# A macaron encoder layer in split float32: the order of the matmul passes inside the FFN's block products

## The chip, the cores and the metric

The kernel runs on one core of a Trainium2 chip. A core has a matrix engine (TensorE, PE in the profile, with a separate row PEld for loading its stationary operand), a vector engine (DVE), a scalar engine (ACT), a general engine (POOL), and queues that start transfers (SP's above all). Matmul results go to PSUM, eight banks of 512 float32 per partition; everything else works from the on-chip SBUF, which is loaded from HBM by DMA. The engines run side by side, each through its own queue in order, and wait for each other by semaphores.

The metric is the device time of one execution in microseconds (us), and lower is better. Times come from runs of the same program; a profile is one further execution, recorded instruction by instruction.

## The reference

One layer on 256 frames of width 2048, all in float32:

```python
def swiglu(h, w1, w3, w2):
    return (jax.nn.silu(h @ w1) * (h @ w3)) @ w2
...
x = x + 0.5 * swiglu(rmsnorm(x, ffn1_norm_g[l]), ffn1_w1[l], ffn1_w3[l], ffn1_w2[l])
h = rmsnorm(x, mix_norm_g[l])
proj = h @ w_in[l]
...
merged = jax.nn.sigmoid(ga) * (y_a @ w_branch_a[l]) + jax.nn.sigmoid(gb) * (y_b @ w_branch_b[l])
x = x + merged @ w_out[l]
x = x + 0.5 * swiglu(rmsnorm(x, ffn2_norm_g[l]), ffn2_w1[l], ffn2_w3[l], ffn2_w2[l])
```

The inner width of the FFN is 5632. Between the two FFNs stand two attention branches (differential attention and latent attention) and their projections. This case touches only the two FFNs.

## The kernel before

**Precision.** A float32 product is made from three passes of TensorE. Every operand is split into a high part in the format `fp32r` and a low part, the remainder (`split`, L118 to L121: ACT casts the high part, L120; DVE subtracts it from the source, L121). A product adds high times high, high times low and low times high into the same accumulator. Activations are split once, ahead of time (`T[:, 0]` is the high part and `T[:, 1]` the low part, the stationary operands); weights are split as they arrive.

**Blocks.** The FFN's matrices are multiplied in 2 x 2 blocks by `gemm2` (L293). One call computes a 256 x 1024 result as four blocks of 128 x 512, and adds up over *pairs* of 128-deep slices of the inner dimension. A pair is of one of two kinds:

- "S": seven products of 128 x 128 by 128 x 512 instead of eight (Strassen's scheme in Winograd's form, the table `SEVEN`, L253). It needs sums of weight blocks, which DVE makes (L318 to L320), and two splits: `s`, of the four blocks themselves (one sum takes the place of one of them), and `w`, of three sums. 21 passes.
- "P": the plain eight products (`PLAIN`, L255), arranged so that they go into four of the same accumulators. One split, `p`. 24 passes.

The seven accumulators `q1` to `q7` are one PSUM bank each; the eighth bank is for transposes. `q1`, `q6` and `q7` get products of S pairs only, so they are emptied right after the last S pair of the call (L335 to L343); `q5`, `q2`, `q3` and `q4` are emptied after the last pair (L346 to L355), by DVE operations of 512 columns that add them into the SBUF tile `ev` or, in the last down calls, into `x`.

**Buffers of weights.** A pair's weights come by two DMAs of 512 KB each on SP's queue into a tile `raw` (L313, L314); there are three `raw` tiles, three `wh` (high) and three `wl` (low). An S pair uses one `raw` and two of each of the others. A `raw` tile is free when its pair's split is done.

**Order of passes.** The helper `three` (L303) issues the three passes of one product one after another: high-high, high-low, low-high. The program gives the instructions this order and a planner may move an instruction ahead of others whose operands are not ready in the planner's own reckoning; what an engine really runs is seen in the trace.

**Calls.** `ffn` (L378) goes over 11 groups of 512 inner columns. Each group makes one *up* call over the eight pairs of the width (kinds `TKINDS` = P S P P S P S P, L359): `w1` and `w3` together, then Silu (ACT, L394) and the multiplication (DVE, L395). The result is put into the list `pend` as small steps to be transposed (`put_pairs`, L260: two `turn` steps that transpose on PE, then `sums`, which makes the sums and splits of the stationary operands); `gemm2` runs one such step after each pair, and all that are left before pair number `due`. After groups 2, 5, 8 and 10 two *down* calls follow, for the two halves of the output (`DOWN`, L362: the groups 0-2, 3-5, 6-7, 8-10; two pairs each, of kinds `GKINDS`). The results of the first three are added to `x_mid` in HBM by a POOL DMA with accumulation (L415); the last adds them onto the `x` that was loaded back (`load_x`, L385).

So each FFN has 11 up calls and 8 down calls, and the whole kernel 38 calls of `gemm2`.

## Time and profile before

| | us |
|---|---|
| median of 3 runs | 2462.64 (2459.66 to 2463.09) |
| the profiled execution | 2461.4 |
| its span | 2459.6 |
| first FFN, from the first to the last weight pass in its PE rows | 11.9 to 749.0 |
| second FFN, the same | 1722.8 to 2454.8 |

How the rows are read: PE's matmul rows overlap, because a matmul starts while the one before still drains; a 512-column pass is shown as 0.39 us long while the next starts 0.227 us later. A busy PE is therefore not PE at its peak, and a loss shows as a larger distance of starts or as the idle time in brackets at the end of a row, with the instruction that ended it. In the groups, the number behind the second bar is the idle time of the engine directly before instructions of that group. In the windows the columns are length, busy time of each engine with its count of instructions, then the granted TensorE clock (1.00 is full), the busy share of the DMA engines and GB/s. The tiles are named by the call: `f_u_...` belongs to up calls, `f_d_...` to down calls; `hp`, `lp`, `hs`, `ls`, `hw`, `lw` are the high and low parts of the splits `p`, `s` and `w`.

### The profile page before, as it was taken

Reading aid. Unit: us, or ns where it says so; the run is one execution under the profiler, and the core shown is the slowest. Engines: PE = TensorE matmul, PEld = TensorE weight load, DVE = VectorE, ACT = ScalarE, POOL = GpSimd, SP = SyncE. Lnnn points to the kernel's source line nnn. Section 1 sums busy time; section 2 is a strip of 40 time slices with the busy share of each in tenths; the row PEclk is TensorE's granted clock in tenths of the full one; section 3 lists DMA queues with packets and bytes.
Section 4 is the critical chain, followed back from the end, with each engine's and each line's share of the span. In section 5 each row is a group of like instructions: output and inputs, shape, how many; then the busy total and the mean of one; then the engine's idle time right before and its main releaser. Section 6 shows DMA issues by size and latency. Waiting matters only on the chain.

```text
span 2459.6 us, 28650 instructions
## 1 busy us (share of the span) xinstructions
PE 2401.8 (98%) x10788; PEld 1956.4 (80%) x10788; DVE 1866.9 (76%) x2363; ACT 1241.1 (50%) x1290; POOL 133.8 (5%) x177
## 2 busy tenths in 40 slices
PE   7999999999999999999999999999999999999999
PEld 6887887787888888888878878888777787788787
DVE  7987887888896666756665664556888898788798
ACT  5554554554554455545545544444554455455453
POOL 2000000000000100001121210000000000000000
PEclk9999999999999999999999999999999999999999
DMA  7567567567675555555454445565656665756765
GB/s 245 185 198 226 194 197 211 193 201 206 204 237 178 187 171 171 171 158 170 142 169 146 153 160 184 188 229 195 211 192 205 206 200 178 220 195 199 207 221 171
DMA packets 240490, 471.88 MB, mean 192 GB/s; under 512 B 15012, under 2 KB 28000, under 8 KB 240096
## 3 DMA queue, kind: packets, MB, share of 16 engines
q1 hardware_dynamic: 233280, 446.30, 55.8%
q0 software_dynamic: 6064, 23.10, 4.1%
q8 instruction: 85, 1.39, 0.2%
q10 hardware_dynamic: 1008, 0.66, 0.1%
q14 instruction: 53, 0.43, 0.0%
HBM read 449.02 MB, written 20.97 MB: 191 GB/s over the span
## 4 chain that ended last, share of the span: by engine, by line
PE 25%; issue 23%; POOL 2%; DVE 2%; ACT 1%; DMA 1%; POOLq 0%; SPq 0%; DVEq 0%; ACTq 0%
PE f_u_q L305 3%; PE f_d_q L305 2%; PE ms L557 1%; PE wo L161 1%; PE wo L159 1%; PE wo L160 1%; PE bb L160 1%; PE bb L159 1%; PE bb L161 1%; PE gb L160 1%; PE gb L159 1%; PE gb L161 1%; PE ba L159 1%; PE ba L160 1%; PE ba L161 1%
## 5 line engine op out<-in xcount | busy, mean ns | idle before, releaser
L305 PE MATMUL f_d_q<-f_d_hp,f_gp 128*128 128x512 f32 x960 | 306.7, 395 | 1.6 <-DVE f_u_e L348 1.5
L120 ACT CAST f_u_hp<-f_u_w 128x2048 fp32r<-128x2048 f32 x110 | 210.4, 1912 | 148.3 <-PE f_u_q L305 90.9
L305 PE MATMUL f_u_q<-f_u_hp,hT1p 128*128 128x512 f32 x880 | 283.5, 395 | 0.8 <-ACT f_u_hp L120 0.6
L305 PE MATMUL f_u_q<-f_u_hp,hT2p 128*128 128x512 f32 x880 | 279.9, 391 | 1.5 <-DVE f_u_e L348 0.9
L121 DVE TENSOR_TENSOR f_u_lp<-f_u_w,f_u_hp 128x2048 fp32r<-128x2048 f32 x110 | 251.5, 2286 | 38.5 <-ACT f_u_hp L120 38.5
L120 ACT CAST f_u_hs<-f_u_w 128x2048 fp32r<-128x2048 f32 x66 | 126.1, 1911 | 190.4 <-DVE f_u_w L319 161.9
L305 PEld LDWEIGHTS f_d_q<-f_d_hp,f_gp 128*128 128x128 f32 x960 | 182.3, 190 | 41.7 <-issue 4.0
L305 PE MATMUL f_d_q<-f_d_lp,f_gp 128*128 128x512 f32 x480 | 190.6, 397 | 15.5 <-DVE f_d_lp L121 15.4
L121 DVE TENSOR_TENSOR f_u_ls<-f_u_w,f_u_hs 128x2048 fp32r<-128x2048 f32 x66 | 151.2, 2292 | 62.3 <-ACT f_u_hs L120 62.3
L305 PEld LDWEIGHTS f_u_q<-f_u_hp,hT1p 128*128 128x128 f32 x880 | 167.1, 190 | 38.4 <-issue 2.9
L305 PEld LDWEIGHTS f_u_q<-f_u_hp,hT2p 128*128 128x128 f32 x880 | 165.0, 188 | 38.7 <-issue 4.1
L305 PE MATMUL f_u_q<-f_u_lp,hT1p 128*128 128x512 f32 x440 | 174.2, 396 | 7.3 <-DVE f_u_lp L121 7.3
L305 PE MATMUL f_u_q<-f_u_lp,hT2p 128*128 128x512 f32 x440 | 172.5, 392 | 6.6 <-DVE f_u_lp L121 6.5
L120 ACT CAST f_d_hp<-f_d_w 128x2048 fp32r<-128x2048 f32 x60 | 114.8, 1913 | 63.4 <-PE f_d_q L305 36.6
L121 DVE TENSOR_TENSOR f_d_lp<-f_d_w,f_d_hp 128x2048 fp32r<-128x2048 f32 x60 | 136.9, 2285 | 12.0 <-ACT f_d_hp L120 11.9
L305 PEld LDWEIGHTS f_d_q<-f_d_lp,f_gp 128*128 128x128 f32 x480 | 91.5, 191 | 39.3 <-DVE f_d_lp L121 20.7
L121 DVE TENSOR_TENSOR f_u_lw<-f_u_s,f_u_hw 128x1536 fp32r<-128x1536 f32 x66 | 115.6, 1751 | 0.0
L120 ACT CAST f_d_hs<-f_d_w 128x2048 fp32r<-128x2048 f32 x28 | 53.6, 1913 | 110.5 <-DVE f_d_w L319 85.0
L305 PEld LDWEIGHTS f_u_q<-f_u_lp,hT1p 128*128 128x128 f32 x440 | 83.6, 190 | 29.0 <-DVE f_u_lp L121 12.1
L305 PEld LDWEIGHTS f_u_q<-f_u_lp,hT2p 128*128 128x128 f32 x440 | 82.6, 188 | 27.2 <-DVE f_u_lp L121 10.7
L159 PE MATMUL da<-da_h,hTm 128*128 128x512 f32 x256 | 104.2, 407 | 0.0
L121 DVE TENSOR_TENSOR da_l<-da_w,da_h 128x1024 fp32r<-128x1024 f32 x64 | 76.6, 1221 | 34.6 <-ACT da_h L120 34.3
(385 smaller groups left out, 5673.3 us busy)
## 6 DMA issues: line engine op xcount, KB each, us to landing
f_u_w<-in_ffn_w SPq DMA_DIRECT2D x352, 512.0 KB, 4.7
f_d_w<-in_ffn_w SPq DMA_DIRECT2D x176, 512.0 KB, 5.0
da_w<-in_w_in SPq DMA_DIRECT2D x64, 512.0 KB, 4.5
dav_w<-in_w_in SPq DMA_DIRECT2D x32, 512.0 KB, 4.5
ga_w<-in_w_in SPq DMA_DIRECT2D x32, 512.0 KB, 4.4
ba_w<-in_w_branch_a SPq DMA_DIRECT2D x32, 512.0 KB, 4.9
gb_w<-in_w_in SPq DMA_DIRECT2D x32, 512.0 KB, 4.5
bb_w<-in_w_branch_b SPq DMA_DIRECT2D x32, 512.0 KB, 4.6
```

The lines of the kernel that those rows point to most:

```text
L120: nc.scalar.copy(out=hi, in_=src)
L121: nc.vector.tensor_sub(out=lo, in0=src, in1=hi.bitcast(F32))
L159: nc.tensor.matmul(out=o, lhsT=hi(kb, t), rhs=wh[:, j], start=first, stop=False)
L160: nc.tensor.matmul(out=o, lhsT=hi(kb, t), rhs=wl[:, j], start=False, stop=False)
L161: nc.tensor.matmul(out=o, lhsT=lo(kb, t), rhs=wh[:, j], start=False, stop=last)
L305: nc.tensor.matmul(out=q[o], lhsT=x, rhs=b, start=o not in started, stop=end)
L557: nc.tensor.matmul(out=sp[:, c0:c1], lhsT=q[:, qc:qc + P], rhs=k[:, 0:n], start=i == 0, stop=i == len(blocks) - 1)
```

## The change

It changes only the two FFNs. The count of matmuls, the weight bytes and the splits stay the same.

1. *Passes of a pair.* The helper `passes` takes all products of a pair. Except for the pairs noted, it issues first all passes with the high part of the weights (high-high and low-high of every product) and then all passes with the low part. In an S pair it does so for the four `s` products and then for the three `w` products. The first pair of a call, and a last pair of kind P, go product by product, as before, though with the low part of the weights third.
2. *Accumulators emptied 1024 wide.* `q2` and `q3` become the two halves of one two-bank tile `q23` and are added in one operation; where the result stays in `ev`, the two subtractions from `q5` become one operation.
3. *Pairs reordered.* Up calls other than an FFN's first run in the order `UP` (S P P S P S P P); `GKINDS` becomes PS, SP, PP, with group 7 kept as two P pairs; in a down call the first S pair is moved to the front (S P S P P P, S P P P, and S P P P S P for the last).
4. *Transposes.* A `wait` step in front of `put_pairs` moves each of its steps behind one more pair. The first half of `x` is loaded at once, no longer as steps of `pend`.

```diff
-                split(T[:, 0], T[:, 1], g[:, :n])
+                split(T[:, 0, :n], T[:, 1, :n], g[:, :n])
...
-        q = {k: pools["acc"].tile([P, NW], F32, tag=k, bufs=1, name=f"{name}_{k}") for k in ("q1", "q2", "q3", "q4", "q5", "q6", "q7")}
+        q = {k: pools["acc"].tile([P, NW], F32, tag=k, bufs=1, name=f"{name}_{k}") for k in ("q1", "q4", "q5", "q6", "q7")}
+        q23 = pools["acc"].tile([P, 2, NW], F32, tag="q23", bufs=1, name=f"{name}_q23")
+        q["q2"], q["q3"] = q23[:, 0], q23[:, 1]
...
-        def three(o, T, slot, bh, bl, stop):
-            for x, b, end in ((T[:, 0, slot], bh, False), (T[:, 0, slot], bl, False), (T[:, 1, slot], bh, stop)):
-                nc.tensor.matmul(out=q[o], lhsT=x, rhs=b, start=o not in started, stop=end)
+        nS = sum(p[0] == "S" for p in pairs)
+        left = {o: 3 * nS + (6 * (n - nS) if o in ("q2", "q3", "q4", "q5") else 0) for o in q}
+
+        def passes(T, prods, in_turn):
+            high = lambda o, s, bh, bl: [(o, T[:, 0, s], bh), (o, T[:, 1, s], bh)]
+            low = lambda o, s, bh, bl: [(o, T[:, 0, s], bl)]
+            todo = [m for p in prods for f in (high, low) for m in f(*p)] if in_turn else \
+                [m for f in (high, low) for p in prods for m in f(*p)]
+            for o, x, b in todo:
+                left[o] -= 1
+                nc.tensor.matmul(out=q[o], lhsT=x, rhs=b, start=o not in started, stop=left[o] == 0)
                 started.add(o)
...
-                for o, slot, b, u in SEVEN:
-                    three(o, T, slot, B[b][0][:, u], B[b][1][:, u], o in ("q1", "q6", "q7") and i == lastS)
+                for part in (("sw",) if i == 0 else ("s", "w")):
+                    passes(T, [(o, slot, B[b][0][:, u], B[b][1][:, u]) for o, slot, b, u in SEVEN if b in part], i == 0)
...
-                for o, slot, right_side in [(o, s, 1 - l) for o, s, l in PLAIN]:
-                    for j in range(2):
-                        u = 3 * j if right_side else 1 + j
-                        three(o, T, slot + j, ph[:, u], pl[:, u], i == n - 1 and j == 1)
+                units = [(o, slot + j, 1 + j if l else 3 * j) for o, slot, l in PLAIN for j in range(2)]
+                passes(T, [(o, slot, ph[:, u], pl[:, u]) for o, slot, u in units], i in (0, n - 1))
...
-        nc.vector.tensor_sub(out=e12, in0=q["q5"], in1=e12)
         if x is None:
-            nc.vector.tensor_sub(out=e22, in0=q["q5"], in1=e21)
-            x11, x12, x21 = e11, e12, e21
+            nc.vector.tensor_tensor(out=ev[:, :, NW:], in0=q["q5"].unsqueeze(1).to_broadcast([P, 2, NW]),
+                                    in1=ev.rearrange("p t n -> p (t n)")[:, NW:3 * NW].rearrange("p (a n) -> p a n", a=2),
+                                    op=ALU.subtract)
+            x1, x21 = ev[:, 0], e21
         else:
+            nc.vector.tensor_sub(out=e12, in0=q["q5"], in1=e12)
...
-        nc.vector.tensor_add(out=x11, in0=q["q2"], in1=x11)
-        nc.vector.tensor_add(out=x12, in0=q["q3"], in1=x12)
+            x1 = x[:, 0]
+        nc.vector.tensor_add(out=x1, in0=q23.rearrange("p a n -> p (a n)"), in1=x1)
...
-    TKINDS, GKINDS = "PSPPSPSP", ("PS", "PP", "SP")
+    TKINDS, GKINDS = "PSPPSPSP", ("PS", "SP", "PP")
+    UP = (1, 0, 2, 4, 3, 6, 5, 7)
...
-            ev = gemm2(rows(w1, g * NW), rows(w3, g * NW), T, f"{name}_u{g}", due=5 if g == 0 else None)
+            ev = gemm2(rows(w1, g * NW), rows(w3, g * NW), [T[i] for i in UP] if g else T, f"{name}_u{g}", due=5 if g == 0 else None)
...
-            later(*put_pairs(G[g], lambda t, ev=ev: ev[:, t, 0:NW], None, f"{name}{g}"))
+            if g == 7:
+                G[g] = [("P", v, kb) for _, v, kb in G[g]]
+            later(wait, *put_pairs(G[g], lambda t, ev=ev: ev[:, t, 0:NW], None, f"{name}{g}"))
...
-                pend[0:0] = [partial(load_x, t, 0) for t in range(NT)]
+                for t in range(NT):
+                    load_x(t, 0)
...
             pairs = [p for i in DOWN[g] for p in G[i]]
+            pairs.insert(0, pairs.pop([p[0] for p in pairs].index("S")))
```

The tile of the FFN's stationary operands (`ffn_T`) is also written so that P pairs beyond five would lie behind the S pairs; there are five, so nothing moves.

More of the change, by code (lines that the diff above doesn't have):

```diff
@@ L288, in sums, with gemm2 @@
                     n = 6
-                split(T[:, 0], T[:, 1], g[:, :n])
+                split(T[:, 0, :n], T[:, 1, :n], g[:, :n])
         return [partial(turn, t) for t in range(NT)] + [sums]
-    def gemm2(left, right, pairs, name, due=None, x=None):
-        q = {k: pools["acc"].tile([P, NW], F32, tag=k, bufs=1, name=f"{name}_{k}") for k in ("q1", "q2", "q3", "q4", "q5", "q6", "q7")}
+    def gemm2(wleft, wright, pairs, name, due=None, x=None):
+        q = {k: pools["acc"].tile([P, NW], F32, tag=k, bufs=1, name=f"{name}_{k}") for k in ("q1", "q4", "q5", "q6", "q7")}
+        q23 = pools["acc"].tile([P, 2, NW], F32, tag="q23", bufs=1, name=f"{name}_q23")
+        q["q2"], q["q3"] = q23[:, 0], q23[:, 1]
         ev = pools["ev"].tile([P, NT, 2 * NW], F32, tag="ev", bufs=1, name=f"{name}_e")
@@ L312, in gemm2 @@
             raw = wtile("raw", F32, f"{name}_w")
-            nc.sync.dma_start(out=raw[:, 0::3], in_=right(k))
-            nc.sync.dma_start(out=raw[:, 1:3], in_=left(k))
+            nc.sync.dma_start(out=raw[:, 0::3], in_=wright(k))
+            nc.sync.dma_start(out=raw[:, 1:3], in_=wleft(k))
             h4 = lambda m: (wtile("wh", F32R, f"{name}_h{m}"), wtile("wl", F32R, f"{name}_l{m}"))
@@ L370, in ffn_T @@
         nP = len(TKINDS) - nS
-        tS = pair_views(big.tile([P, nS * 14, P], F32R, tag=tagS, name=f"{name}s"), nS, 7)
-        tP = pair_views(big.tile([P, nP * 12, P], F32R, tag=tagP, name=f"{name}p"), nP, 6)
+        n1, n2 = min(nP, 5), max(nP - 5, 0)
+        b1 = big.tile([P, nS * 14 + n2 * 12, P], F32R, tag=tagS, name=f"{name}s")
+        tS, tP = pair_views(b1, nS, 7), pair_views(b1[:, nS * 14:], n2, 6)
+        tP += pair_views(big.tile([P, n1 * 12, P], F32R, tag=tagP, name=f"{name}p"), n1, 6)
         return [(k, v, 2 * i) for i, (k, v) in enumerate(with_kinds(TKINDS, tS, tP))]
```

## The prediction, made before the changed kernel was run

> **What bounds the kernel now.** I read the page's busy times, then its costliest groups, then the busy times of single calls of `gemm2`, then the order of time around one stall.
>
> ```profile
> span 2459.6 us, 28650 instructions
> PE 2401.8 (98%) x10788; PEld 1956.4 (80%) x10788; DVE 1866.9 (76%) x2363; ACT 1241.1 (50%) x1290; POOL 133.8 (5%) x177
> ...
> L305 PE MATMUL f_d_q<-f_d_lp,f_gp 128*128 128x512 f32 x480 | 190.6, 397 | 15.5 <-DVE f_d_lp L121 15.4
> ...
> L305 PE MATMUL f_u_q<-f_u_lp,hT1p 128*128 128x512 f32 x440 | 174.2, 396 | 7.3 <-DVE f_u_lp L121 7.3
> L305 PE MATMUL f_u_q<-f_u_lp,hT2p 128*128 128x512 f32 x440 | 172.5, 392 | 6.6 <-DVE f_u_lp L121 6.5
> ```
>
> PE is the bound. What it loses in the FFNs stands in front of the low passes (rows with `lp` as moving operand): 15.5 + 7.3 + 6.6 = 29.4 us of idle time, released by the DVE subtraction that makes the low part (L121). No other L305 group loses more than 2 us. So a reorder can win only where PE stands still; the number of matmuls stays the same.
>
> The pitch of an undisturbed stream comes from two rows of the order of time; between them lie 12 matmuls (each product is high, low, high):
>
> ```profile
> 395.85 0.39 PE L305 MATMUL f_d_q<-f_d_lp,f_gp 128*128 128x512 f32 x1
> ...
> 398.57 0.39 PE L305 MATMUL f_d_q<-f_d_lp,f_gp 128*128 128x512 f32 x1
> ```
>
> 2.72 / 12 = 0.2267 us. An up call has 183 matmuls (3 S pairs of 21, 5 P pairs of 24): 41.5 us. A down call over six pairs has 138: 31.3 us; over four pairs 93: 21.1 us. Against this stand the calls by busy time (L305 alone). First the second down pass of each group set and the up call behind it, 12 calls in both FFNs; then, as a second answer, all other up calls but the two first; then the two first:
>
> ```profile
> 382.85:417.48 34.63, 32.07 (x140) 25.59 (x138) 1.00 0.72 214
> 417.48:462.24 44.76, 42.35 (x184) 34.11 (x184) 1.00 0.72 212
> 570.61:596.26 25.65, 23.41 (x94) 18.36 (x93) 0.93 0.77 220
> ...
> sum 455.85, PE 429.93 PEld 344.92; mean PE 35.83 PEld 28.74
> ```
> ```profile
> 639.26:682.13 42.87, 42.48 (x184) 34.12 (x184) 1.00 0.61 203
> ...
> sum 605.94, PE 597.14 PEld 474.67; mean PE 42.65 PEld 33.90
> ```
> ```profile
> 11.92:66.62 54.70, 49.31 (x183) 36.60 (x184) 0.97 0.69 241
> 1722.83:1768.23 45.40, 43.12 (x183) 33.83 (x184) 1.00 0.66 217
> ```
>
> The 12 calls have 4 x 138 + 2 x 93 + 6 x 183 = 1836 matmuls, 416.2 us by the pitch; they take 455.85, so **39.6 us are lost, 3.3 a call**. The 14 others take 605.94 against 14 x 41.5 = 580.9: 25 us, 1.8 a call, and about 0.9 of that are their eight transposes, which the 12 do not have. The calls that lose much are those after a down pass. Why, shows one of them:
>
> ```profile
> 398.14 1.23 DVE L318 TENSOR_TENSOR f_d_s<-f_d_w 128x1024 f32<-128x1024 f32 x1 [4.46 <-DMA f_d_w<-in_ffn_w]
> ...
> 398.79 0.61 PE L305 MATMUL f_d_q<-f_d_hp,f_gp 128*128 128x512 f32 x2
> 399.29 2.29 DVE L121 TENSOR_TENSOR f_d_lp<-f_d_w,f_d_hp 128x2048 fp32r<-128x2048 f32 x1
> 401.49 0.69 DVE L319 TENSOR_TENSOR f_d_w<-f_d_s,f_d_w 128x512 f32<-128x512 f32 x1
> ...
> 401.63 0.50 PE L305 MATMUL f_d_q<-f_d_lp,f_gp 128*128 128x512 f32 x1 [2.22 <-DVE f_d_lp L121]
> ```
> ```profile
> f_d_w<-in_ffn_w SPq DMA_DIRECT2D x6, 512.0 KB, 6.5
> f_u_w<-in_ffn_w SPq DMA_DIRECT2D x6, 512.0 KB, 4.3
> x_mid<-f_d_e POOLq DMA_DIRECT2D x1, 1024.0 KB, 10.7
> ```
> ```profile
> PE f_d_q L305 <- DVE f_d_lp L121: 15.4, 11, 2.8
> ```
>
> After each down pass POOL adds 1 MB into `x_mid` (L415). Beside it the weight loads land after 6.5 us, not 4.3 (the DMA rows of 383 to 412 us). In DVE's queue the sums of the next S pair (L318) stand ahead of this P pair's low part; they wait 4.46 us for their load, the low part waits behind them, and PE, which has run two high passes, stands still for 2.2 us. The load itself is not late for its own pair; it is late for the one queued behind it. The last row, from the view of waits, gives the worst case: 11 such waits of PE in the down calls, the longest 2.8 us.
>
> **The change part by part.**
>
> *High passes first.* A P pair that is neither first nor last now gives PE 16 high passes, 16 x 0.2267 = 3.6 us, before it needs the low part; today it has one or two. The longest wait for a low part, 2.8 us, fits in. In an S pair eight high passes come first (1.8 us), then four low ones. The high tile is also free eight passes earlier, 1.8 us, for ACT's next cast. *Pairs reordered:* each call but the two first up calls starts with its S pair, so the S load that was late (fifth of six) is now first and third. A load is issued when DVE is through with the pair three before it (three `raw` tiles), so both S loads are asked for before the store begins; beside it load the late P pairs, which PE reaches two to three pairs, over 10 us, later. Of the 39.6 us I leave 0.7 a call for its first pair and what is late next (a first S pair that waits for DVE): 8.4. **Term a: -31 us.**
>
> The first up call has the same stall inside (30.71 us, 1.83 idle), and a slow clock behind it. The third number from the end is the granted clock:
>
> ```profile
> 32.10:35.50 3.40, 3.40 (x10) 2.62 (x9) 3.33 (x4) 0.03 (x1) 0.00 (x0) 0.50 0.94 332
> ...
> 2107.40:2110.80 3.40, 3.40 (x9) 2.62 (x9) 2.01 (x3) 2.89 (x2) 0.00 (x0) 0.50 0.69 208
> 401.60:405.00 3.40, 3.37 (x15) 2.78 (x16) 1.99 (x3) 2.67 (x2) 0.00 (x0) 1.00 0.60 195
> ```
> ```profile
> 30.71 0.50 PE L305 MATMUL f_u_q<-f_u_lp,hT1p 128*128 128x512 f32 x1 [1.83 <-DVE f_u_lp L121]
> ...
> 2107.21 0.65 PE L305 MATMUL f_d_q<-f_d_lp,f_gp 128*128 128x512 f32 x1 [2.68 <-DVE f_d_lp L121]
> ```
>
> A 3.4 us stretch at half clock costs 1.7 us. Stall and stretch give **term b: -3.5 us**. The stretches of the 12 calls are inside term a already. [...]
>
> *Ordinary call starts.* The first pair now begins with q1, q6, q7, emptied long before, where it began with q5, emptied last. I take 0.1 us a call off the 20 calls that are not in a: **term c: -2 us**.
>
> *Accumulators 1024 wide.* Before, each is one operation of 512:
>
> ```profile
> L346 DVE TENSOR_TENSOR f_d_e<-f_d_q,f_d_e x16: 680/682/692, 182.8 to 2451.2; 128x512 f32<-128x512 f32 x16
> ```
>
> Two of them take 1.36 us, one 1024 wide 1.23 by L318's row above (from SBUF; a 1024-wide read of PSUM is not in the trace; bounds 0.68 and 1.36). In 34 calls two are saved, in four one: 72 x 0.13 = 9 us of DVE. DVE is 76% busy and these run beside the last passes, so 0 on the path. If the cover goes (the last call), 0.3 us either way. q2's bank is now held until q3 is read too; the next S pair needs q2 only as its fifth product, 12 passes (2.7 us) in: 0.
>
> *Transposes one pair later.* They stop waiting for the activation at a call's start, but a down call needs the last group's operands at its fifth pair. Today the chain runs:
>
> ```profile
> 361.60 0.60 ACT L272 ACTIVATE pf_f<-tp_f 128x512 f32<-128x512 f32 x1
> ...
> 367.09 1.08 DVE L121 TENSOR_TENSOR f_gs<-pf_f,f_gs 128x896 fp32r<-128x896 f32 x1
> ```
>
> 6.6 us from the second transpose to the last low part, with one pair more to spare. After the change one P pair, 24 x 0.2267 = 5.4 us, lies between: 0 to 1.2 us late, in six calls. I take 0.5: **term d: +3 us**. The x loads issued at once, and group 7 kept as P pairs, move nothing that PE waits for: the loads land a whole call ahead, and the pair counts stay 5 P and 3 S, 4 P and 2 S, 3 P and 1 S: 0. The part between the FFNs is not touched.
>
> Sum: -31 - 3.5 - 2 + 3 = -33.5. The profiled execution took 2461.4 us, 1.8 outside its span; 2461.4 - 33.5 = 2428. The median of the runs is 2462.64, 1.2 above it: **2429 us**.
>
> **The rivals.**
>
> 1. *All small waits go too.* Then the 12 calls end near the pitch (-38), the 14 up calls lose half of what is not transposes (-6), b and the down calls add -6: 2462.6 - 50 = **2412**. For it: DVE has no wait left in front of it. Against: first and last pairs still run product by product.
> 2. *The wait only moves.* The last pair of a call runs in turn, so it has no 3.6 us; if the next S pair's L318 stands ahead of its low part as above, half of term a stays (-16), c goes, d costs its upper end (6 x 1.2 = +7) and b -3.5, starts +0: about -13, **2449**. Against: by then the store has ended.
> 3. *Slower: S first starves every call's start.* An S pair needs 1.23 + 2 x 0.69 + 2.29 + 1.75 = 6.6 us of DVE before its last low part, and at a call's start DVE empties accumulators first. The first row, of the page's groups, has the last summand; the others show a call that begins with S today:
>
> ```profile
> L121 DVE TENSOR_TENSOR f_u_lw<-f_u_s,f_u_hw 128x1536 fp32r<-128x1536 f32 x66 | 115.6, 1751 | 0.0
> ...
> 2388.44 0.69 DVE L354 TENSOR_TENSOR f_u_e<-f_u_q,f_u_e 128x512 f32<-128x512 f32 x1
> ...
> 2389.05 2.28 DVE L121 TENSOR_TENSOR f_d_ls<-f_d_w,f_d_hs 128x2048 fp32r<-128x2048 f32 x1
> ...
> 2391.39 0.50 PE L305 MATMUL f_d_q<-f_d_ls,f_gs 128*128 128x512 f32 x1 [0.27 <-DVE f_d_ls L121]
> ```
>
> The subtraction ran behind L354 and PE lost 0.27 us, after hoisting six high passes. 36 calls will start so. It decides from 33.5 / 36 = 0.93 us a call; at the whole 2.28 us it is +82 - 33.5: **2511**. Against: before a call's start now lie two or three P pairs, 2.29 us of DVE each against 5.4 of PE, where here lay one.
> 4. *Nothing happens.* PE's rows show high passes hoisted already, so the order that runs is not the order written; if it comes out alike, **2462**.
> 5. *Banks.* Low passes now change the accumulator on nearly every pass. If that made PE idle in gaps and halved its clock, each 3.4 us stretch would cost 1.7; 20 of them eat the gain, 40 give **2496**. Today's S pairs change accumulators every one to three passes with the pitch unbroken. [...]
>
> **How the numbers follow.** Forecast 0.52, rival 1 0.18, rival 2 0.15, rival 3 0.06, rival 4 0.06, rival 5 0.03. 0.2% of this kernel, 4.9 us, is about what a measurement can tell from no change. Faster: 0.52 + 0.18 + 0.15 = 0.85; same 0.06; slower 0.09. The range reaches from below rival 1 to above rival 2, 2408 to 2452, and leaves out 3 to 5 and a tail of 1.
>
> **What would show it.** Right: idle in front of `lp` under 5 us in all; the 12 calls at about 32, 42.2 and 21.8 us; half-clock stretches gone from both FFNs but the first microseconds. Wrong: idle of a microsecond in front of `ls` at call starts (3), in front of `lp` of last pairs (2), in front of the fifth pair of a first down pass (d), or a granted clock under 1 without a stall before it (5). The forecast falls if the weight loads after the store land so late that 3.6 us do not cover them.

## The result, and the profile after

The changed kernel took 2418.96 us (median of 4 runs, 2417.49 to 2419.36) beside 2461.84 us for the kernel before on the same chip (4 runs, 2459.66 to 2463.09): a ratio of 0.9826, 95% interval 0.9809 to 0.9843, so 43 us less. The prediction was 2429, with a range of 2408 to 2452.

From the page of the changed kernel, its span, the busy times and the groups of low passes that carried the argument before; its matmul line is now L316:

```profile
span 2417.2 us, 28714 instructions
PE 2380.4 (98%) x10788; PEld 1958.0 (81%) x10788; DVE 1860.7 (77%) x2291; ACT 1241.8 (51%) x1290; POOL 129.9 (5%) x177
...
L316 PE MATMUL f_d_q<-f_d_lp,f_gp 128*128 128x512 f32 x448 | 128.9, 389 | 0.0
L316 PE MATMUL f_u_q<-f_u_lp,hT1p 128*128 128x512 f32 x440 | 122.5, 391 | 1.2 <-DVE f_u_lp L121 1.2
L316 PE MATMUL f_u_q<-f_u_lp,hT2p 128*128 128x512 f32 x440 | 122.3, 390 | 0.3 <-DVE f_u_lp L121 0.3
```

The number behind the second bar is PE's idle time in front of the group: 15.5 + 7.3 + 6.6 us before, 0.0 + 1.2 + 0.3 now. PE executes the same 10788 matmuls; 32 of the down calls' 480 low passes, those of group 7, are now in a group of their own, without idle time. The 12 calls after (or beside) an accumulating store, matmul line alone; the columns are the window, its length, PE's and the weight loads' busy time, the granted clock, the DMA share and GB/s:

```profile
181.88:213.16 31.28, 31.28 (x140) 25.90 (x139) 1.00 0.85 255
213.16:254.64 41.48, 41.48 (x185) 34.35 (x184) 1.00 0.71 216
373.87:405.15 31.28, 31.28 (x140) 25.91 (x138) 1.00 0.81 244
405.15:446.63 41.48, 41.48 (x185) 34.36 (x183) 1.00 0.69 209
555.50:576.58 21.08, 21.08 (x94) 17.45 (x93) 1.00 0.71 200
576.58:620.88 44.30, 42.51 (x184) 34.04 (x183) 1.00 0.70 214
...
sum 421.18, PE 418.18 PEld 344.01; mean PE 34.85 PEld 28.67
```

A second down pass of six pairs takes 31.28 us and an up call 41.48: exactly the pitch (138 and 183 times 0.2267), PE busy from end to end. In the first FFN, shown here, five of the six calls run so; the up call behind the short down pass still loses something (44.30). All twelve went from 455.85 to 421.18 us, **34.7 of the 42.4 us** that the span lost.

PE's waits inside the FFNs that are left, from the view of waits (total, times, longest):

```profile
PE f_u_q L316 <- DVE f_u_e L366: 7.3, 8, 1.5
...
PE f_u_q L316 <- ACT f_u_hs L120: 2.1, 2, 1.4
PE f_u_q L316 <- DVE f_u_lp L121: 1.6, 2, 1.2
```

The first is new. L366 empties q4, the last accumulator of a call. The order of time around one of these waits shows why it comes late:

```profile
448.16 1.23 DVE L365 TENSOR_TENSOR f_u_e<-f_u_q,f_u_e 128x1024 f32<-128x1024 f32 x1
...
450.62 1.23 DVE L329 TENSOR_TENSOR f_u_s<-f_u_w 128x1024 f32<-128x1024 f32 x1 [1.24 <-DMA f_u_w<-in_ffn_w]
...
451.77 0.68 DVE L366 TENSOR_TENSOR f_u_e<-f_u_q,f_u_e 128x512 f32<-128x512 f32 x1
...
452.50 0.73 PE L316 MATMUL f_u_q<-f_u_hw,hT1s 128*128 128x512 f32 x2 [1.40 <-DVE f_u_e L366]
```

It is the old mechanism with another victim. In DVE's queue the sums of the next S pair (L329) stand ahead of q4's emptying; they wait 1.24 us for their load, q4 waits behind them, and PE loses 1.40 us at the next call's first product with q4. DVE's own waiting has not become less, only harmless nearly everywhere. In front of the first sums of an S pair it waited 24.9 us for the loads of the up calls and 20.5 us for those of the down calls; now it is 75.3 and 1.1 us:

```profile
L329 DVE TENSOR_TENSOR f_u_s<-f_u_w 128x1024 f32<-128x1024 f32 x66 | 80.6, 1221 | 75.3 <-DMA f_u_w<-in_ffn_w 75.3
```

Nor do the loads beside a store land sooner, 7.0 us here and 6.5 before (the view of DMA, 374 to 404 us); the second down pass of that stretch loses nothing by it:

```profile
f_d_w<-in_ffn_w SPq DMA_DIRECT2D x4, 512.0 KB, 7.0
x_mid<-f_d_e POOLq DMA_DIRECT2D x1, 1024.0 KB, 9.3
```

### The profile page after: what moved, and what is told of

Same layout as the page of the kernel before. It is cut to its first block, busy times and chain, and to the rows that moved or that the text cites. A ratio compares the mean times of both kernels' runs of the same rounds, so it can differ in the third digit from the quotient of the medians.

```text
span 2417.2 us, 28714 instructions
## 1 busy us (share of the span) xinstructions
PE 2380.4 (98%) x10788; PEld 1958.0 (81%) x10788; DVE 1860.7 (77%) x2291; ACT 1241.8 (51%) x1290; POOL 129.9 (5%) x177
## 4 chain that ended last, share of the span: by engine, by line
PE 42%; DVE 5%; DMA 3%; POOL 2%; issue 1%; ACT 1%; SPq 0%; DVEq 0%; ACTq 0%; POOLq 0%
PE f_u_q L316 15%; PE f_d_q L316 7%; DMA f_u_w<-in_ffn_w 2%; PE ms L575 1%; PE wo L161 1%; PE wo L159 1%; PE wo L160 1%; PE bb L159 1%; PE bb L161 1%; PE bb L160 1%; PE gb L160 1%; PE gb L159 1%; PE gb L161 1%; PE ba L159 1%; PE ba L160 1%
## 5 line engine op out<-in xcount | busy, mean ns | idle before, releaser
L316 PE MATMUL f_d_q<-f_d_hp,f_gp 128*128 128x512 f32 x896 | 233.0, 391 | 0.0
L316 PE MATMUL f_u_q<-f_u_hp,hT1p 128*128 128x512 f32 x880 | 225.6, 393 | 0.9 <-ACT f_u_hp L120 0.9
L316 PE MATMUL f_u_q<-f_u_hp,hT2p 128*128 128x512 f32 x880 | 222.8, 390 | 0.5 <-ACT f_u_hp L120 0.5
L316 PEld LDWEIGHTS f_d_q<-f_d_hp,f_gp 128*128 128x128 f32 x896 | 167.2, 188 | 35.3 <-DVE f_gp L121 0.8
L316 PEld LDWEIGHTS f_u_q<-f_u_hp,hT1p 128*128 128x128 f32 x880 | 165.4, 189 | 36.1 <-ACT f_u_hp L120 1.8
L316 PEld LDWEIGHTS f_u_q<-f_u_hp,hT2p 128*128 128x128 f32 x880 | 164.6, 188 | 34.9 <-ACT f_u_hp L120 0.8
L329 DVE TENSOR_TENSOR f_u_s<-f_u_w 128x1024 f32<-128x1024 f32 x66 | 80.6, 1221 | 75.3 <-DMA f_u_w<-in_ffn_w 75.3
L316 PE MATMUL f_d_q<-f_d_lp,f_gp 128*128 128x512 f32 x448 | 128.9, 389 | 0.0
L316 PE MATMUL f_u_q<-f_u_lp,hT1p 128*128 128x512 f32 x440 | 122.5, 391 | 1.2 <-DVE f_u_lp L121 1.2
L316 PE MATMUL f_u_q<-f_u_lp,hT2p 128*128 128x512 f32 x440 | 122.3, 390 | 0.3 <-DVE f_u_lp L121 0.3
L120 ACT CAST f_u_hw<-f_u_s 128x1536 fp32r<-128x1536 f32 x66 | 97.6, 1479 | 43.1 <-DVE f_u_s L331 32.3
L159 PE MATMUL da<-da_h,hTm 128*128 128x512 f32 x256 | 104.2, 407 | 0.0
L161 PE MATMUL da<-da_h,hTm 128*128 128x512 f32 x256 | 100.2, 391 | 0.0
L160 PE MATMUL da<-da_l,hTm 128*128 128x512 f32 x256 | 99.9, 390 | 0.0
```

The lines of the kernel that those rows point to most:

```text
L120: nc.scalar.copy(out=hi, in_=src)
L159: nc.tensor.matmul(out=o, lhsT=hi(kb, t), rhs=wh[:, j], start=first, stop=False)
L160: nc.tensor.matmul(out=o, lhsT=hi(kb, t), rhs=wl[:, j], start=False, stop=False)
L161: nc.tensor.matmul(out=o, lhsT=lo(kb, t), rhs=wh[:, j], start=False, stop=last)
L316: nc.tensor.matmul(out=q[o], lhsT=x, rhs=b, start=o not in started, stop=left[o] == 0)
L329: nc.vector.tensor_tensor(out=sm[:, 0:2], in0=raw[:, 0:1].to_broadcast([P, 2, NW]), in1=raw[:, 1::2], op=ALU.add)
```

## The experiments

The theory behind the prediction: the store into `x_mid` makes a weight load late, the sums of an S pair wait for it at the head of DVE's queue, and a P pair's low part waits behind them; high passes first cover that wait, and the new order of pairs moves the late load away from it. Rivals: the order of the pairs costs that much with any load, store or not; or the gain comes from the other edits (the transposes one pair later, the loads of x at once, the wide emptying).

All readings stand in one table, in us. Each column is the sum row of the windows of one set of calls, matmul line alone: the 12 calls, the 14 other up calls, the two first up calls, and the two first down passes of the last group set ("last down"). The changed kernel stands twice, from two profiled runs; they differ by up to 2.3 us in a column of calls and by 2.6 us in the span, so less than that is not read as an effect. The ratio is to the kernel before on the same chip. The runs were not all on one chip, and the kernel before took 2457.7 to 2463.3 us (medians) beside them, so differences of a few us between spans are uncertain: by the spans runs 5, 7 and 8 are 2 to 9.5 us longer than the changed kernel, by the ratios 8 to 12 us, where the interval of a ratio reaches 4 to 6 us to either side.

| kernel | span | 12 calls | 14 up calls | first two | last down | ratio, 95% interval |
|---|---|---|---|---|---|---|
| before | 2459.6 | 455.9 | 606.0 | 100.1 | 66.7 | 1 |
| after | 2417.2 | 421.2 | 607.6 | 95.0 | 65.4 | 0.9826, 0.9809 to 0.9843 |
| after, again | 2414.6 | 419.4 | 605.3 | 95.0 | 66.1 | 0.9816, 0.9799 to 0.9834 |
| 1 before, no store | 2427.3 | 423.8 | 606.4 | 100.1 | 66.7 | one run, 2429.1 us |
| 2 before, high passes first | 2443.7 | 431.2 | 603.1 | 96.6 | 86.1 | 0.9937, 0.9918 to 0.9956 |
| 3 before, new order of pairs | 2456.1 | 428.2 | 602.6 | 104.3 | 82.1 | 0.9989, 0.9978 to 1.0000 |
| 4 before, high first, x at once | 2426.7 | 431.6 | 603.4 | 96.2 | 67.4 | 0.9865, 0.9841 to 0.9889 |
| 5 after, in turn | 2419.1 | 432.1 | 596.7 | 95.0 | 65.2 | 0.9862, 0.9843 to 0.9880 |
| 6 after, old order of pairs | 2449.8 | 428.9 | 614.2 | 95.8 | 80.2 | 0.9966, 0.9952 to 0.9980 |
| 7 after, loads of x late | 2424.1 | 418.9 | 605.1 | 94.6 | 77.7 | 0.9864, 0.9838 to 0.9890 |
| 8 after, no step of waiting | 2422.0 | 418.6 | 617.5 | 93.9 | 65.1 | 0.9859, 0.9838 to 0.9881 |
| 9 after, all emptied 512 wide | 2414.6 | 422.8 | 596.6 | 98.9 | 65.7 | 0.9834, 0.9812 to 0.9856 |
| 10 after, q2 and q3 in own banks | 2412.8 | 422.8 | 596.5 | 99.7 | 65.9 | 0.9819, 0.9803 to 0.9836 |
| 11 after, high first in three pairs | 2428.1 | 443.5 | 597.8 | 93.7 | 65.5 | 0.9874, 0.9852 to 0.9896 |

**1. Is the store the cause?** The kernel before without its accumulating store; it leaves out the sums into `x_mid` of the down calls of the first three group sets.

```diff
-                    nc.gpsimd.dma_start(out=xdram[:, :, ns], in_=ev, accum_op=ALU.add)
+                    pass
```

> The kernel before without the accumulating store of the first three down passes of both FFNs (it leaves out that sum into x_mid). Theory A (the prediction's: the store beside the weight loads makes them late): weight loads in the second down passes land after 4 to 5 us, not 6.5; the 12 calls (six second down passes and the six up calls behind them) lose less than 12 us over their pitch, where they lost 39.6; span 25 to 35 us shorter, 2425 to 2435. Theory B (the order of the pairs is at fault, with any load): the 12 calls lose 30 us or more, and the span is within 8 us of 2460.

The same stretch of 383 to 412 us that showed loads of 6.5 us before, in the view of DMA:

```profile
f_u_w<-in_ffn_w SPq DMA_DIRECT2D x8, 512.0 KB, 4.4
f_d_w<-in_ffn_w SPq DMA_DIRECT2D x4, 512.0 KB, 4.5
```

At the head of DVE's queue the sums of the S pair waited 4.46 us for their load; at the same place it is now:

```profile
391.95 1.22 DVE L318 TENSOR_TENSOR f_d_s<-f_d_w 128x1024 f32<-128x1024 f32 x1 [1.77 <-DMA f_d_w<-in_ffn_w]
```

And the groups of low passes on its page:

```profile
L305 PE MATMUL f_d_q<-f_d_lp,f_gp 128*128 128x512 f32 x480 | 188.0, 392 | 2.3 <-DVE f_d_lp L121 1.9
...
L305 PE MATMUL f_u_q<-f_u_lp,hT1p 128*128 128x512 f32 x440 | 173.7, 395 | 2.2 <-DVE f_u_lp L121 2.2
L305 PE MATMUL f_u_q<-f_u_lp,hT2p 128*128 128x512 f32 x440 | 172.0, 391 | 1.4 <-DVE f_u_lp L121 1.4
```

With the code and the order of the pairs untouched, PE's idle time there falls from 29.4 to 5.9 us and the 12 calls from 455.9 to 423.8; the other columns move by less than half a microsecond. So the store is the cause, and the order of the pairs alone is not. The changed kernel gets the same gain with the store in place.

The edit takes away two things at once, though: the store's traffic beside the loads, and its hold on `ev`, of which there is one buffer. In ten of the 12 calls the order of time of the kernel before shows the late load in front of the stall. In the two short second down passes (570.61 and 2277.85) it shows the hold: ACT's emptying of q1 into `ev` waits until the store from it has ended, DVE's next emptying waits for ACT, and the P pair's low part stands behind both:

```profile
581.00 0.59 ACT L336 COPY f_d_e<-f_d_q 128x512 f32<-128x512 f32 x1 [2.24 <-DMA x_mid<-f_d_e]
581.62 0.69 DVE L337 TENSOR_TENSOR f_d_e<-f_d_q,f_d_e 128x512 f32<-128x512 f32 x1 [2.05 <-ACT f_d_e L336]
582.23 2.28 DVE L121 TENSOR_TENSOR f_d_lp<-f_d_w,f_d_hp 128x2048 fp32r<-128x2048 f32 x1
...
584.57 0.50 PE L305 MATMUL f_d_q<-f_d_lp,f_gp 128*128 128x512 f32 x1 [2.24 <-DVE f_d_lp L121]
```

Without the store these two calls go from 25.65 and 25.60 us to 21.96 and 21.97, 7.3 of the 32 us. In the changed kernel ACT waits there even longer, 7.6 us in the two calls, and PE no longer notices: both take 21.08.

**2 and 3. Each main edit alone, in the kernel before.** High passes first (the function `passes` and its calls, nothing else), and the new order of pairs (`GKINDS`, `UP`, the S pair first in a down call, group 7 as P pairs):

```diff
-                for o, slot, b, u in SEVEN:
-                    three(o, T, slot, B[b][0][:, u], B[b][1][:, u], o in ("q1", "q6", "q7") and i == lastS)
+                for part in (("sw",) if i == 0 else ("s", "w")):
+                    passes(T, [(o, slot, B[b][0][:, u], B[b][1][:, u]) for o, slot, b, u in SEVEN if b in part], i == 0)
...
+                units = [(o, slot + j, 1 + j if l else 3 * j) for o, slot, l in PLAIN for j in range(2)]
+                passes(T, [(o, slot, ph[:, u], pl[:, u]) for o, slot, u in units], i in (0, n - 1))
```

> The kernel before with one part of the change: passes with the high part of the weights first; old pair order, accumulators emptied 512 wide, transposes not delayed. Theory (a stall is a late S load queued ahead of the low part, and 3.6 us of high passes cover it): the 12 calls after a store keep under 1 us each of their 3.3, the whole is 25 to 35 us under before (2427 to 2437). Rival (the new pair order did it, by asking for the S loads before the store begins): under 10 us gained, idle in front of lp still above 15 us.

```diff
-    TKINDS, GKINDS = "PSPPSPSP", ("PS", "PP", "SP")
+    TKINDS, GKINDS = "PSPPSPSP", ("PS", "SP", "PP")
+    UP = (1, 0, 2, 4, 3, 6, 5, 7)
...
+            pairs.insert(0, pairs.pop([p[0] for p in pairs].index("S")))
```

> The kernel before with the pair order alone (UP, GKINDS, S pair to the front); passes product by product as before. Theory: the order alone also takes the late S load away from the low part, so 15 to 30 us are gained, but call starts on an S pair cost 0.3 to 0.5 us each, 10 to 18 us in 36 calls, net 0 to 20 us (2442 to 2462). Rival (order does it all): 35 us or more gained. Rival (order does nothing for the stall): slower than before by 5 to 20 us.

In the 12 calls each edit alone does most of the work: 24.7 us from the passes (455.9 to 431.2) and 27.7 from the order (to 428.2), 34.7 both together. They cure the same wait twice over. Neither expectation came true as it was argued. High passes first keeps 1.25 us a call where under 1 was expected, and gains 16.6 us, not 25 to 35. The new order lies in its range of 0 to 20 us by luck: the starts on an S pair, which were to eat its gain, cost nothing (602.6 beside 606.0 in the 14 up calls), and something else ate it. Each edit alone opens a hole elsewhere: the two last first down passes go from 66.7 to 86.1 and 82.1 us. The view of waits of the kernel with high passes first names it:

```profile
PE f_d_q L313 <- ACT f_gp L120: 15.0, 2, 8.3
```

PE waits, up to 8.3 us at a time, for the last group's own operands. The last transposes end just where that wait begins, and the sums and splits behind them are still to come:

```profile
2385.38 0.60 PE L173 MATMUL tp_f<-ident,f_u_e 128*128 128x128 f32 x4
...
2392.97 0.41 DVE L287 TENSOR_TENSOR pf_f<-pf_f 128x256 f32<-128x256 f32 x1
...
2394.30 6.51 PE L313 MATMUL f_d_q<-f_d_hp,f_gp 128*128 128x512 f32 x16 [8.32 <-ACT f_gp L120]
```

The small steps (`pend`) are let out one behind each pair; in the last group the two loads of x stand at the head of that list and take the places of the first two pairs. In the kernel before this is not seen (66.7 us for two calls of 31.3 by the pitch, with 16 transposes in them): with the same list, its transposes ran 4.4 to 7.0 us into the call of the second FFN, against 16.5 to 23 us here. Why they ran ahead of their places there and not here is not shown.

**4. The timetable of the small steps.** High passes first and the loads of x at once, in the kernel before:

```diff
-                pend[0:0] = [partial(load_x, t, 0) for t in range(NT)]
+                for t in range(NT):
+                    load_x(t, 0)
```

> The kernel before with the high passes first (that part alone took 2441, and lost 22 us over the pitch in the two last first down passes, 8.7 and 13.1) and, besides, the two loads of x issued at once. Theory A (the timetable of the small steps: without the two loads the last group's transposes come two pairs earlier): those two calls lose under 2 us each, and the time falls by 16 to 20 us, to 2421 to 2426, near the whole change. Theory B (their operands are late for another reason, the queue of ACT and DVE at the call's start): within 4 us of 2441.

The hole closes (86.1 to 67.4), nothing else in the table moves by more than 0.4 us, and the ratio goes from 0.9937 to 0.9865: these two edits alone give most of the change's gain. **7** is the converse, the changed kernel with the loads of x back at the head of the list:

> The changed kernel, with the two loads of x for the last down passes put at the head of the list of small steps again (as before the change), where each takes the place of one step behind a pair. Theory A (the small steps are a timetable: the two loads push the last group's transposes two pairs back, so its operands come late in the two last first down passes): the stall of 6.4 us that the kernel before with the new pair order alone showed there, behind the third pair, comes back in both FFNs, the two calls lose 6 to 9 us each, and the time is 12 to 18 us above the changed kernel, about 2433. Theory B (the loads sit where nothing waits for them): within 2 us of the changed kernel, about 2419.

The two calls go from 65.4 to 77.7, 12.3 us, with PE waiting again in front of operands of the last group:

```profile
PE f_d_q L316 <- ACT f_gs L120: 6.5, 2, 3.4
```

The span grew by 6.9 us only; the rest came back in small amounts in other calls, of the size by which two profiles of the changed kernel differ. Theory A was right on the place and on the two calls (6.1 us each), and the time rose by less than the 12 to 18 us that it said: 6.9 us by the span, 9.5 beside the second profile.

**5 and 6. The same two edits taken out of the full change.** All passes product by product again, and the old order of pairs again:

```diff
-                for part in (("sw",) if i == 0 else ("s", "w")):
-                    passes(T, [(o, slot, B[b][0][:, u], B[b][1][:, u]) for o, slot, b, u in SEVEN if b in part], i == 0)
+                for part in ("sw",):
+                    passes(T, [(o, slot, B[b][0][:, u], B[b][1][:, u]) for o, slot, b, u in SEVEN if b in part], True)
...
-                passes(T, [(o, slot, ph[:, u], pl[:, u]) for o, slot, u in units], i in (0, n - 1))
+                passes(T, [(o, slot, ph[:, u], pl[:, u]) for o, slot, u in units], True)
```

> The changed kernel with every pair product by product (high, high, low), the rest of the change kept. Theory: P pairs lose their 3.6 us of cover; with the new order the store meets no S load, so 5 to 20 us are lost (2424 to 2439), in front of lp and ls. Rival (high first did it all): back to within 5 us of before. Rival (order did it all): within 4 us of the changed kernel.

> The changed kernel with the old pair order; high passes first, 1024-wide emptying and delayed transposes kept. Theory: stalls on lp stay covered, so within 12 us of the changed kernel (2419 to 2431); the 7.3 us of PE's waits for the emptying of q4 at S-first calls go, some waits for q5 at P-first calls come. Rival (order did it): 20 us or more slower than the changed kernel.

With the new order in place, product by product costs 10.9 us in the 12 calls (421.2 to 432.1) and **earns 10.9 in the 14 other up calls** (607.6 to 596.7); the span is 1.9 to 4.5 us longer than the changed kernel's two. So high passes first, inside the full change, are worth some 2 to 5 us by the spans, near the rival that the order does it all, and 9 to 11 by the ratios, inside the theory's 5 to 20. For the old order the theory (within 12 us) missed, and the rival's number (20 or more) came true, but not its reason, that the order alone removes the stalls: PE waits for P pairs' low parts only 1.8 us in all without it. Taking the order out costs 32.6 us of span, yet in the 12 calls no more than 7.7: the rest is in the last down passes (+14.8), the other up calls (+6.6) and calls outside the table. The old order with high passes first is not bad by itself (4 shows it). Beside 4 this kernel has the transposes one pair later and the wide emptying, and its largest wait of PE is again for the last group's operands, 8.1 us in two waits; that points to the transposes, but neither was taken out of this kernel alone.

**8. The step of waiting** that puts a group's transposes one pair later, taken out (`later(wait, *put_pairs(...))` to `later(*put_pairs(...))`):

> The changed kernel without the empty step that puts a group's transposes one pair later, so they follow a call's first pair, as before. Theory A (the empty step keeps PE's transposes from waiting for the activation): each of the 22 calls that carry transposes lets PE wait for ACT or DVE at its start, 0.2 to 0.8 us a call, +4 to +18 us, 2423 to 2437. Theory B (the calls' first S pair is long enough to hide the activation; the prediction's term d had the step cost 0.5 us in six calls): 0 to -3 us, 2416 to 2419.

The 14 up calls lose 9.9 us (607.6 to 617.5), and PE waits in front of the transposes for the product behind the activation (L409), which it does not do in the changed kernel:

```profile
PE tp_f L173 <- DVE f_u_e L409: 11.2, 8, 1.8
```

The span grew by 4.8 us, and by 7.4 beside the second profile of the changed kernel: about what theory A said, and the waits are its waits. The step earns its place.

**9 and 10. The wide emptying.** First everything 512 wide again, with seven tiles of a bank each; then only q2 and q3 so, with q5 still emptied 1024 wide:

```diff
-        q23 = pools["acc"].tile([P, 2, NW], F32, tag="q23", bufs=1, name=f"{name}_q23")
-        q["q2"], q["q3"] = q23[:, 0], q23[:, 1]
...
-        nc.vector.tensor_add(out=x1, in0=q23.rearrange("p a n -> p (a n)"), in1=x1)
+        nc.vector.tensor_add(out=x11, in0=q["q2"], in1=x11)
+        nc.vector.tensor_add(out=x12, in0=q["q3"], in1=x12)
```

> The changed kernel with the accumulators emptied 512 wide again. Theory A (the prediction's: the 9 us of DVE that the wide form saves lie beside the last passes): within 3 us of the changed kernel, 2417 to 2422. Theory B (the emptying of a call's accumulators stands in front of the operations that the next call waits for, so 0.13 us of DVE twice a call is paid): 34 x 0.26 = 9 us more, 2428. Theory C (a bank of its own for q2 is free earlier, and the wait for q4 gets shorter): 3 to 7 us less, 2412 to 2416.

> The changed kernel with q2 and q3 in banks of their own again, emptied 512 wide each; q5 stays emptied 1024 wide. Theory A (the joined tile holds q4 up: q2 and q3 can only be emptied together when q3 is done, which puts q4's emptying last, behind the first sums of the next S pair, which wait for their load): PE's eight waits for q4's emptying, 7.3 us in all, go, and so do the 1 to 2 us that the up calls of the middle of a group set lose; 6 to 10 us faster than the changed kernel, 2409 to 2413. Theory B (with q4 free PE waits in the same place for the S pair's own parts, which hang on the same load): less than 3 us faster, 2416 to 2419. Theory C (22 times 0.14 us more of DVE is paid): 3 us slower, 2422.

Beside the last one the changed kernel was run once more:

> The changed kernel once more, beside the next one. Within 0.15% of 2419.

Neither differs from the changed kernel in time: 2417.2 and 2416.7 us beside 2419.0 and 2416.4. But inside, much moves. With own banks q4's emptying stands in front of the next S pair's sums in DVE's queue; of the 7.3 us of waits for it behind up calls nothing is left (behind a down call one of 1.7 us stands), and the 14 up calls take 596.5 us, 11.1 less. That is theory A's mechanism, with theory B's time: the two first up calls give back 4.7 us and the 12 calls 1.6, and one first down pass 1.5. In the kernel with own banks PE's largest waits in the FFNs are now these, in front of S pairs' parts; others of up to 1.7 us stand in front of an emptying, a transpose and an S pair of a down call:

```profile
PE f_u_q L314 <- ACT f_u_hs L120: 4.5, 3, 2.0
...
PE f_u_q L314 <- DVE f_u_lw L121: 2.6, 2, 1.4
```

What differs is the order in the queues: around 450 us DVE runs q4's emptying (L366, 451.77) behind the next sums (L329, 450.62) in the changed kernel, and with all emptied 512 wide in front of them (L363 at 453.62, L327 at 454.22); why it falls out worse elsewhere stays open.

**11. A mixture of the two orders of passes.** High passes first in the down calls and in the first three pairs of the up calls of groups 0, 3, 6 and 9; product by product elsewhere (a parameter `until` of `gemm2`):

```diff
-                for part in (("sw",) if i == 0 else ("s", "w")):
+                for part in (("sw",) if i == 0 or i >= until else ("s", "w")):
...
-                passes(T, [(o, slot, ph[:, u], pl[:, u]) for o, slot, u in units], i in (0, n - 1))
+                passes(T, [(o, slot, ph[:, u], pl[:, u]) for o, slot, u in units], i in (0, n - 1) or i >= until)
```

> The changed kernel with the high passes first only where the store is near: in the down calls as before, in the up calls of groups 0, 3, 6 and 9 in their first three pairs; all other up pairs run product by product. Theory A (high passes first earns only beside the store, 15.9 to 5.0 us of loss in the 12 calls, and costs elsewhere, because it lets DVE take the next S pair's first sums in front of q4's emptying: the 14 other up calls lose 14.6 us with it and 3.7 without): both gains together, the 14 calls lose 4 us, the 12 about 5, 10 us less than the changed kernel, about 2407 (2404 to 2411). Theory B (the waits for the emptying come from the joined tile alone, whatever the passes' order, or what is saved comes back as another wait, as it did with the banks of their own): 2415 to 2420.

The 14 other up calls did as expected (597.8). But the 12 rose to 443.5, all of it in the six up calls, which take 276.2 us beside 253.9 in the changed kernel: at the fifth pair of each PE waits 2.0 to 2.5 us, and behind the wait the clock is halved in five of them (mean granted clock of the call 0.96, in the sixth 1.00). The order of time, 18 to 24 us into one of them:

```profile
230.48 1.23 DVE L329 TENSOR_TENSOR f_u_s<-f_u_w 128x1024 f32<-128x1024 f32 x1 [3.83 <-DMA f_u_w<-in_ffn_w]
...
233.08 2.29 DVE L121 TENSOR_TENSOR f_u_lp<-f_u_w,f_u_hp 128x2048 fp32r<-128x2048 f32 x1
...
235.42 0.50 PE L316 MATMUL f_u_q<-f_u_lp,hT1p 128*128 128x512 f32 x1 [2.02 <-DVE f_u_lp L121]
```

The very mechanism of the prediction, two pairs past the boundary: a P pair, then an S pair whose load is late. Three pairs' loads had been asked for within 6 us, between 219.28 and 225.01, while the store, issued at 216.00 and 9.2 us on its way, was still running. The DMA of 223 to 233 us, as share of its engines in 40 slices and the loads' landing time:

```profile
DMA  8999899999999999999999999999999999953000
...
f_u_w<-in_ffn_w SPq DMA_DIRECT2D x4, 512.0 KB, 6.9
```

So theory A was right on where high passes first cost and wrong on where they are needed: the pairs whose loads were asked for beside the store come later than the third. How much of the delay is the store's, and how much comes from three pairs' loads so close together, is not separated. Nor is the missing cover the whole cause: in run 5, where no pair has cover, the same sums wait 2.49 us for their load (229.56), PE's waits for `f_u_lp` come to 6.5 us in the whole kernel beside 13.4 here, and the six calls take 259.9 us. Why the mixture is slower there than either order alone stays open. A boundary at five pairs, which would take this one in, was not tried.

## Why the prediction was right, step by step

*The cause and term a (forecast -31, measured -34.7).* Right, place and size, except that in two of the 12 calls the stall came from the store's hold on `ev` and not from a late load (run 1); the cover of high passes works on both. Without the store the 12 calls take 423.8 us; with the change 421.2 and 419.4. Of the 8.4 us that I left, 5.0 are there (421.2 against 416.2 by the pitch). What the term did not see: it is not a sum over the two edits. Each alone brings 25 to 28 us there, and the second adds 7 to 10.

*Term b (-3.5, measured -5.1).* Right: the two first up calls go from 100.1 to 95.0, and the first of them has its clock back (third number from the end, 0.97 before):

```profile
12.02:62.58 50.56, 46.59 (x184) 35.01 (x184) 1.00 0.71 253
```

The kernel before has four half-clock stretches in the FFNs' calls: at 32.1 and 2107.4 us (0.50, the prediction's rows), and from 585.0 and 2291.7 us on (0.51 over 3.5 us), inside the calls at 570.61 and 2277.85 with their mean clock of 0.93. None is left there: the first up call and all 12 calls of the changed kernel have 1.00.

*Term c (-2, measured +1.6 and, in the second profile, -0.7).* This step failed. "The first pair now begins with q1, q6, q7, emptied long before" is true, and the accumulator that came late was q4, the last one, behind L329 in DVE's queue (7.3 us of waits). The 14 calls can do 9 to 11 us better, as 5, 9 and 10 show (596.5 to 596.7), though 9 and 10 lose it again elsewhere. The count was off too: 24 calls outside term a start with an S pair, not 20.

*Wide accumulators (0).* Right in sum, by luck: the wait for q4 is paid back by what other calls lose without the wide form (the two first up calls 3.9 to 4.7 us in 9 and 10), and that loss is not explained. The size was right (L365 takes 1.23 us in the row above, as taken from L318); that the DVE time saved is worth nothing is not shown apart from these. "q2's bank is now held until q3 is read too ... 0" looked at q2 only; it is q4, third in the same queue, that pays 7.3 us.

*Transposes one pair later (+3).* The cost did not occur. In front of the last group's operands in a first down pass PE waits once, 0.2 us (0.9 in the second profile), and the two last down passes of the table are together 0.5 to 1.3 us shorter than before. Run 8 shows what the step does instead: without it PE waits 11.2 us in front of the transposes. The sentence weighed only what the delay costs at a down call, not what it saves at a call's start ("they stop waiting for the activation").

*The loads of x at once ("move nothing that PE waits for: 0").* Right in the sum by luck, wrong in the reason. They do sit on PE's path, through the timetable of the small steps: late, they cost 12.3 us in two calls (run 7), and with high passes first alone some 19 us (runs 2 and 4). In the sum they stand at zero because they pay for a debt that the other edits make. The prediction saw neither the debt nor the payment, and without this edit the result would have been near 2425 (run 7).

*The rivals.* Number 1, at 2412, lies nearer to the result (7 us) than the forecast (10 us). Two of its three parts came: the 12 calls are near the pitch (-34.7 where it had -38), and the first two up calls and the first down passes brought 7.5 us where it had 6. The third did not: the 14 up calls, which were to gain 6, did not gain. Number 2's mechanism did occur, in one place, for 1.2 us (615.76, of the waits for `f_u_lp` above): the last pair in turn. Number 3's did not: the waits for `ls` at call starts are under a microsecond each. Number 4 is out, since the time fell. Of number 5 nothing is seen: the mean granted clock of the whole run is 0.999, and the second down passes of six pairs run at the pitch (31.28 us). The 9 us by which the change did better than the forecast's sum (42.4 of span against 33.5) are term a (3.7), term b (1.6), and all that lies outside the first three columns of calls, which gave 4.2 us (2.4 of them the eight first down passes) where term d took 3; term c took 3.6 of that back.

## What to carry to other kernels

In a queue that runs in order, look for an operation that waits for a transfer and stands ahead of work for something else (here L318 waited 4.46 us, and PE 2.22 us behind it); the victim is named in the waits, the culprit is the row before it. A cover of 3.6 us of independent matmuls and a transfer asked for earlier cured the same wait here, so their gains did not add (24.7 and 27.7 us alone in the 12 calls, 34.7 together), and each alone opened the next wait (two calls from 66.7 to 86.1 and 82.1 us): price each edit in the kernel that has the others. Where small steps are let out one behind each piece of work, the list is a timetable: here two loads at its head, for which no wait of PE is seen, cost 12.3 us in two calls (run 7).

## What the runs showed of the hardware

*The granted clock fell behind short stalls, and not behind each.* In run 11 stalls of one kind stand at the same place of six up calls. One of 2.02 us is in the rows of run 11 above, at 235.42; here is another, and then the 3.4 us behind each (third number from the end: granted clock):

```profile
2120.63 0.50 PE L316 MATMUL f_u_q<-f_u_lp,hT2p 128*128 128x512 f32 x1 [1.99 <-DVE f_u_lp L121]
```

```profile
236.00:239.40 3.40, 3.40 (x10) 2.63 (x9) 3.23 (x2) 0.00 (x0) 0.00 (x0) 0.50 0.88 283
...
2120.60:2124.00 3.40, 3.37 (x15) 2.80 (x16) 3.40 (x2) 0.47 (x1) 0.00 (x0) 1.00 0.66 204
```

After 2.02 us the clock was halved, after 1.99 us it was not. Yet the length does not decide: in the kernel before it fell behind stalls of 1.83 and 2.68 us (the prediction's rows at 30.71 and 2107.21) and stayed full behind one of 2.22 us (401.63, the window from 401.60) and behind the longest of the FFNs:

```profile
1907.49 0.50 PE L305 MATMUL f_d_q<-f_d_lp,f_gp 128*128 128x512 f32 x1 [2.83 <-DVE f_d_lp L121]
```

```profile
1907.50:1910.90 3.40, 3.40 (x15) 2.83 (x16) 1.99 (x3) 2.70 (x2) 0.00 (x0) 1.00 0.64 198
```

What decides is not shown. PE has 10 matmuls in such a stretch instead of 15, so at half clock it costs over a microsecond beside the stall itself: in the kernel before nine matmuls from 31.97 to 35.62 us took 3.65 us, by the pitch 2.04.

*What an accumulating store does to loads beside it.* Beside one of 1 MB into `x_mid`, 10.7 us from issue to landing, the down calls' weight loads (512 KB each) landed after 6.5 us, without it after 4.5 in the same stretch (383 to 412 us, before and run 1). With all such stores come 32 us of the kernel's time, 7.3 of them in the two calls where the store's hold on its source buffer makes the wait (run 1).
